# An encoder layer in f32 on one core: seven products instead of eight for a second pair in the first half of two output projections

## The chip, the cores and the metric

The kernel runs on one core of a Trainium2 chip. The core has TensorE for matrix products (PE; its weight loads are shown as PEld and overlap), VectorE (DVE), ScalarE (ACT), GpSimd (POOL), and SyncE (SP), which here issues the DMAs. Each has its own queue of instructions; semaphores tie them together. The metric is the device time of one execution in microseconds (us), as the median of several runs.

## The reference

One layer, 256 tokens (`S`), width 2048 (`D`), all in f32:

```python
x = x + 0.5 * swiglu(rms_norm(x, ffn1_norm), w_gate, w_up, w_down)      # width 5632
proj = rms_norm(x, mix_norm) @ w_in
x = x + concatenate([pool_mixer(u), gla_mixer(q, k, v, g, a_lr)]) @ w_out
x = x + mem_cross_attention(rms_norm(x, xattn_norm), rms_norm(mem, mem_norm), w_q, w_kv, w_o)
x = x + 0.5 * swiglu(rms_norm(x, ffn2_norm), w_gate, w_up, w_down)
return rms_norm(x, final_norm)
```

The last steps of mixer and attention are products of a 256 x 2048 matrix with a 2048 x 2048 one: `concatenate(...) @ w_out`, and `o @ w_o` at the end of `mem_cross_attention`. These two are called the output stages here.

## The kernel before

**Precision.** TensorE multiplies in a shortened f32 (`float32r`). Each matrix is therefore split into a high part, rounded by a copy on ACT, and a low part, the rest, by a subtraction on DVE. A product of two such matrices is three matmuls: high by high, high by low, low by high (`products`, line 336). Weights come as raw f32 by DMA and are split on the fly: a plain unit of 128 x 2048 values takes one cast of `wh` from `raw` (line 258, ACT) and one subtraction `wl` (line 259, DVE).

**Units.** The work is a stream of units (`Stream`, line 34): one load of 1 MB of weights, its split, and a function that issues its matmuls. Loads run three units ahead, splits two; `wh` and `wl` have three buffers each, `raw` three. Between units stand other operations (`st.op(f, after)`), each given as a number of units to wait. The order in which instructions are put on each engine's queue is made at build time by a scheduler that plans with estimated durations; `in_turn`, `behind_weights` and `among_weights` (lines 236 to 255) hold chosen operations in order among the weight splits on ACT and DVE.

**Seven products.** `block_s` (line 466) computes a block of 256 tokens x 1024 columns over eight pairs of 128 rows of `k`, one pair a unit. A plain unit (`unit_p`, line 506) does 2 x 2 x 2 quarter products, 24 matmuls of 128 x 512 on line 341. For a pair named in `sevens` a unit (`unit_s`, line 489) does seven quarter products in the way of Strassen and Winograd, 21 matmuls on line 462 (`seven`). It needs sums of the weight quarters and of the activation quarters:

- `split_seven` (line 424) makes three sums of weights on DVE (`T`, line 439: one of 128 x 1024, two of 128 x 512), and splits both raw quarters and sums: casts `xh` (line 258) and `wh` (line 442, two) on ACT, subtractions `xl` (line 259) and `wl` (line 443) on DVE.
- `Sums.make` (line 391) makes the sums of activations on DVE (lines 400 to 412) and splits them into `ye` and a quarter of `ys` (`split`, lines 264 and 265). It overwrites a quarter of `ys`, which `parts` hands to the seven products; plain units of that pair read `ys` as it was, so a pair's sums are made behind the last plain unit that reads it.

Four partial sums (P1, P5, P6, P7) go to two PSUM tiles of their own (`open_parts`, line 484), the others into the block's own two (`open_whole`, line 479); PSUM has four such tiles (line 100). Behind the last seven-unit `combine` (line 520) copies one of the four (line 524, ACT) and adds them up (lines 525, 526 and 529, DVE), and `merge` adds the outcome to x (line 719, twice). At the block's end the residual adds the rest to x (line 707, twice) and x goes to DRAM.

**An output stage** is one call of `into_x` (line 761): two halves of 1024 columns, `b` = 0 and 1, eight units each. It fetches the half's x, runs `block_s` with the orders and sevens of its `way`, and has two `fold`s (line 724) a half, for the 512 columns each: 16 transposes of x on PE into a `px` PSUM tile (line 730), eight scaled splits into `xs` (lines 227 on ACT, 228 on DVE), two squares (line 741). The folds of the first half run among the second half's units; those of the second half run at the start of the block that follows. `w_out` is followed by the attention's first projection, `w_o` by the second FFN.

Three ways exist (lines 755 to 759). `WHOLE` is that of four down projections in the FFNs, which have no folds; `OUTPUT` that of the two output stages; `REST` that of the FFNs' last thirds. A way is: the pairs with sums, how many units behind the call each pair's sums are made, the order of pairs in each half, and which pairs are done with seven products in each half.

Of the kernel before, what the change touches and what calls it, by code (L numbers as in the profile page):

```python
# [90 lines left out]
def build(ctx, tc, I, out):  # L91
# [651 lines left out]
    class IntoX:  # L743
# [7 lines left out]
        def make_sums(self, after=None):  # L751
            for g, n in zip(self.sums.pairs, after or self.after):
# [1 line left out]

    WHOLE = IntoX((0, 4), (2, 5), ((1, 2, 3, 5, 0, 6, 4, 7), (1, 2, 0, 3, 4, 5, 6, 7)),
                  ((0, 4), (0, 4)))
    OUTPUT = IntoX((0, 4), (0, 4), ((1, 2, 3, 4, 0, 5, 6, 7), (1, 2, 0, 3, 4, 5, 6, 7)),
                   ((0,), (0, 4)))
    REST = IntoX((0,), (2,), ((1, 2, 3, 4, 0, 5), None), ((0,), ()), False)

    def into_x(w, act, scale, gain=None, k0=0, nk=KT, spread_too=True, src=None, way=OUTPUT):

        for b in range(2):
            st.op(lambda b=b: fetch_x(b, src), 2)
            cols = wwide(w, b * 2 * NB, k0, nk)
            if way.sevens[b]:
                block_s(cols, act, way.sums, way.orders[b], residual(scale, b, 0),
                        early_parts(scale, b), way.sevens[b])
            else:
                block_t(cols, act, residual(scale, b))  # L770
            if gain is not None:
                for j in range(2):
                    st.op(lambda c=2 * b + j: fold(c, gain), 1)
        if gain is not None:
            st.op(lambda: finish_norm(4, spread_too), 2)
            if spread_too:
                st.op(spread_norm, 3)
# [426 lines left out]
        for j in range(4):  # L1204
            split_scaled(xs, 4 * c + j, v[:, j, :], gcol(G_MEM + 4 * c + j))

    OUTPUT.make_sums((1, 4))
    into_x(I["w_out"][0], ys, 1.0, G_X)
    st.op(mem_in, 2)
    for c in range(4):  # L1210
# [60 lines left out]
    def values(h):  # L1271
        for p in range(2):
            ps = ptile(uid("pv"))
            for d in range(2):
                col = slice((2 * p + d) * P, (2 * p + d + 1) * P)
                parts = [(m, a, b) for m in range(2) for a, b in ((0, 0), (0, 1), (1, 0))]
                for i, (m, a, b) in enumerate(parts):
                    nc.tensor.matmul(  # L1278
                        ps[:, d, :S], xa["V"][:, m, a, col], xa["PT"][:, m, b, :],
                        start=i == 0, stop=i == 5,  # L1280
                    )
            split_pair(ys, 4 * h + 2 * p, ps[:, :, :S])
# [6 lines left out]
    for h in range(H):  # L1289
# [4 lines left out]
        st.op(lambda h=h: values(h), 1)  # L1294
    OUTPUT.make_sums()
    into_x(w_o, ys, 1.0, G_FFN2, spread_too=False)
# [190 lines left out]
def program(shapes):  # L1487
    import concourse.bacc as _bacc

    nc = _bacc.Bacc("TRN2", target_bir_lowering=False, num_devices=1)  # L1490
    args = {
        name: nc.dram_tensor(f"in_{name}", shapes[name], F32, kind="ExternalInput").ap()
        for name in _INS
    }
    out = nc.dram_tensor("out", _OUT, F32, kind="ExternalOutput").ap()
    with tile.TileContext(nc, schedule_with_timeline_sim=True) as tc, ExitStack() as ctx:
        build(ctx, tc, args, out)
    return nc
# [10 lines left out]
```

## Time and profile before

| what | us |
|---|---|
| median of 3 runs (2095.96 to 2096.49) | 2096.08 |
| the profiled execution, in all | 2096.43 |
| its span, first to last instruction | 2094.5 |
| first load of `w_out` issued | 887.7 |
| first load of `w_o` issued | 1269.9 |

Rows of a profile read `start, duration, engine, line, operation, out<-in`, with the shape and the count; `[2.04 <-ACT wh L258]` is the idle time of the engine before the row and what ended it. Buffer numbers are left out of names: `wl` is any of its three buffers. A matmul of 128 x 512 is shown with 0.39 us, but the next starts 0.23 later, since they are pipelined and their ends are modelled. In the chain as pieces a row is `start, us, what` with the count, so us by count is what one costs. In the table of stretches, the columns are the stretch, its length, busy us and count of PE, PEld, DVE, ACT and POOL, the granted share of TensorE's clock, the DMA's busy share, and GB/s.

### The profile page before, as it was taken

How to read it: one execution, taken by the hardware profiler on the slowest of the kernel's cores; microseconds unless marked ns; L12 is line 12 of the kernel's file. 1: busy time of each engine (PE TensorE's matmuls, PEld its weight loads, DVE VectorE, ACT ScalarE, POOL GpSimd, SP SyncE). 2: the span in 40 equal slices, each digit the busy share in tenths (PEclk: the TensorE clock that was granted, in tenths of full speed). 3: DMA queues.
4: the chain of work that ended last, by engine and by line, in shares of the span. 5: the costliest groups of instructions: out<-in, count | busy, mean ns of one | idle time of the engine just before them, and what ended most of it. 6: DMA issues, size and time to landing. Idle time of an engine off the chain costs nothing.

```text
span 2094.5 us, 24553 instructions
## 1 busy us (share of the span) xinstructions
PE 2081.0 (99%) x9901; PEld 1741.6 (83%) x9901; DVE 1729.1 (83%) x1568; ACT 1115.7 (53%) x1096; POOL 14.1 (1%) x41
## 2 busy tenths in 40 slices
PE   9999999999999999999999999999999999999998
PEld 7878888888888888888888888888888888888886
DVE  7999899989998677688665555879998999989974
ACT  7654455644554555365655444556554556545544
POOL 0000000000000000000000000000000000000001
PEclk9999999999999999999999999999999999999999
DMA  7656666566656655467655555656576765676673
GB/s 262 202 199 223 240 221 209 190 224 239 223 198 236 215 179 195 151 197 266 236 181 167 172 164 167 228 190 219 182 239 209 245 205 186 222 240 222 209 255 118
DMA packets 143608, 435.94 MB, mean 208 GB/s; under 512 B 9860, under 2 KB 13544, under 8 KB 143112
## 3 DMA queue, kind: packets, MB, share of 16 engines
q1 hardware_dynamic: 143464, 434.38, 61.5%
q8 instruction: 77, 1.26, 0.2%
q14 instruction: 35, 0.29, 0.0%
q10 hardware_dynamic: 32, 0.01, 0.0%
HBM read 417.58 MB, written 16.78 MB: 207 GB/s over the span
## 4 chain that ended last, share of the span: by engine, by line
PE 93%; DVE 4%; issue 1%; ACT 1%; DMA 0%; SPq 0%; DVEq 0%
PE pt L341 44%; PE pt L462 21%; PE pa L326 15%; PE pb L341 6%; PE pe L341 3%; DVE T L439 1%; PE ph L818 1%; DVE wl L259 1%; DVE wl L443 1%; DVE xl L259 1%; PE pl L1241 1%; PE pv L1278 1%; PE px L730 1%; ACT wh L258 0%; DVE sg L539 0%
## 5 line engine op out<-in xcount | busy, mean ns | idle before, releaser
L259 DVE TENSOR_TENSOR wl<-raw,wh 128x2048 fp32r<-128x2048 f32 (+2 forms) x279 | 626.2, 2249 | 233.6 <-ACT wh L258 232.6
L258 ACT CAST wh<-raw 128x2048 fp32r<-128x2048 f32 (+2 forms) x279 | 523.3, 1880 | 339.5 <-PE pt L341 106.5
L341 PE MATMUL pt<-wh,xs 128*128 128x512 f32 x1536 | 495.0, 390 | 0.0
L341 PE MATMUL pt<-wh,ys 128*128 128x512 f32 x1360 | 427.8, 390 | 0.0
L442 ACT CAST wh<-T 128x1024 fp32r<-128x1024 f32 x206 | 216.8, 1053 | 340.0 <-DVE T L439 325.8
L341 PEld LDWEIGHTS pt<-wh,xs 128*128 128x128 f32 x1536 | 287.6, 188 | 59.4 <-ACT xs L227 0.2
L326 PE MATMUL pa<-xs,wh 128*128 128x512 f32 x896 | 315.9, 397 | 0.0
L341 PE MATMUL pt<-wl,xs 128*128 128x512 f32 x768 | 299.7, 390 | 0.0
L341 PEld LDWEIGHTS pt<-wh,ys 128*128 128x128 f32 x1360 | 255.0, 188 | 52.7
L341 PE MATMUL pt<-wl,ys 128*128 128x512 f32 x680 | 264.9, 390 | 0.0
L326 PE MATMUL pa<-xs,wl 128*128 128x256 f32 x896 | 248.3, 281 | 0.0
L443 DVE TENSOR_TENSOR wl<-T,wh 128x2048 fp32r<-128x2048 f32 x103 | 235.2, 2283 | 1.3 <-ACT wh L442 1.3
L326 PEld LDWEIGHTS pa<-xs,wh 128*128 128x128 f32 x896 | 167.6, 188 | 38.1 <-issue 0.3
L259 DVE TENSOR_TENSOR xl<-raw,xh 128x1536 fp32r<-128x1536 f32 x103 | 180.3, 1750 | 0.0
L326 PEld LDWEIGHTS pa<-xs,wl 128*128 128x128 f32 x896 | 169.1, 189 | 1.7 <-issue 0.2
L341 PEld LDWEIGHTS pt<-wl,xs 128*128 128x128 f32 x768 | 144.2, 188 | 29.8
L258 ACT CAST xh<-raw 128x1536 fp32r<-128x1536 f32 x103 | 152.3, 1479 | 10.6 <-DMA raw<-in_ffn_w_gate 8.5
L341 PEld LDWEIGHTS pt<-wl,ys 128*128 128x128 f32 x680 | 127.7, 188 | 26.2
L439 DVE TENSOR_TENSOR T<-T,raw 128x512 f32<-128x512 f32 x206 | 142.2, 690 | 5.7
L439 DVE TENSOR_TENSOR T<-raw 128x1024 f32<-128x1024 f32 x103 | 125.4, 1217 | 0.5
L462 PE MATMUL pt<-wh,xs 128*128 128x512 f32 x320 | 124.6, 389 | 0.0
L462 PE MATMUL pt<-wh,xe 128*128 128x512 f32 x320 | 124.5, 389 | 0.0
(236 smaller groups left out, 2412.6 us busy)
## 6 DMA issues: line engine op xcount, KB each, us to landing
raw<-in_ffn_w_down SPq DMA_DIRECT2D x88, 1024.0 KB, 5.5
raw<-in_ffn_w_up SPq DMA_DIRECT2D x80, 1024.0 KB, 5.0
raw<-in_ffn_w_gate SPq DMA_DIRECT2D x77, 1024.0 KB, 5.0
raw<-in_w_in SPq DMA_DIRECT2D x32, 1024.0 KB, 5.2
raw<-in_xattn_w_kv SPq DMA_DIRECT2D x32, 1024.0 KB, 5.3
raw<-in_w_out SPq DMA_DIRECT2D x16, 1024.0 KB, 5.6
raw<-in_xattn_w_q SPq DMA_DIRECT2D x16, 1024.0 KB, 5.9
raw<-in_xattn_w_o SPq DMA_DIRECT2D x16, 1024.0 KB, 5.6
```

The source lines that it names most:

```text
L258: in_turn("scalar", lambda: nc.scalar.copy(hi, src))
L259: in_turn("vector", lambda: nc.vector.tensor_tensor(out=lo, in0=src, in1=f32(hi), op=ALU.subtract))
L326: nc.tensor.matmul(o, w, x, start=k == 0 and i == 0, stop=last and i == 1)
L341: nc.tensor.matmul(ps, a, w, start=first and i == 0, stop=last and i == 2)
L439: in_turn("vector", lambda: nc.vector.tensor_tensor(out=o, in0=a, in1=b, op=ALU.add))
L442: in_turn("scalar", lambda: nc.scalar.copy(th[:, c], t[:, c]))
L443: in_turn("vector", lambda: nc.vector.tensor_tensor(out=tl, in0=t, in1=f32(th), op=ALU.subtract))
L462: nc.tensor.matmul(banks[n], x, w, start=n in fresh and j == 0, stop=n in ends and j == 2)
L730: nc.tensor.transpose(v[:, j, h * P : (h + 1) * P], x[:, h, j * P : (j + 1) * P], ident)
L818: nc.tensor.transpose(v[:, i, h * P : (h + 1) * P], g[:, h, i * P : (i + 1) * P], ident)
L1241: nc.tensor.matmul(ps[:, t, :M], ys[:, 4 * h + d, a, tok], xa["K"][:, d, b, :], start=i == 0, stop=i == 11,)
L1278: nc.tensor.matmul(ps[:, d, :S], xa["V"][:, m, a, col], xa["PT"][:, m, b, :], start=i == 0, stop=i == 5,)
```

## The change

```diff
-    OUTPUT = IntoX((0, 4), (0, 4), ((1, 2, 3, 4, 0, 5, 6, 7), (1, 2, 0, 3, 4, 5, 6, 7)),
-                   ((0,), (0, 4)))
+    OUTPUT = IntoX((0, 4), (0, 5), ((1, 2, 3, 5, 0, 6, 4, 7), (1, 2, 0, 3, 4, 5, 6, 7)),
+                   ((0, 4), (0, 4)))
...
-    OUTPUT.make_sums((1, 4))
+    OUTPUT.make_sums((1, 5))
     into_x(I["w_out"][0], ys, 1.0, G_X)
```

In the first half of both output stages pair 4 was a plain unit, the fourth; it becomes a unit of seven products, the seventh of eight. Pair 0 stays the fifth. Pair 4's sums are made one unit later, behind the fifth unit instead of the fourth; in the mixer `make_sums((1, 5))` says so, in attention the way's own `(0, 5)`. The combine of the first half, which follows the last seven-unit, comes behind the seventh unit instead of the fifth. The second half has the same order and sevens as before.

## The prediction

> **What bounds the kernel now.** I read the page's busy shares, its chain that ended last, the chain as pieces in order of time, stretches of 25 us over the mixer's output stage, then that stage instruction by instruction.
>
> ```profile
> PE 2081.0 (99%) x9901; PEld 1741.6 (83%) x9901; DVE 1729.1 (83%) x1568; ACT 1115.7 (53%) x1096; POOL 14.1 (1%) x41
> PE 93%; DVE 4%; issue 1%; ACT 1%; DMA 0%; SPq 0%; DVEq 0%
> ```
>
> PE is the bound, and the chain hardly leaves it. In the stage:
>
> ```profile
> 914.60 21.78 PE pt L341 x96
> ...
> 964.50 1.75 PE px L730 x16
> ...
> 977.60 7.48 PE pt L462 x33
> ```
>
> A product costs 21.78 / 96 = 0.227 us of PE, on line 341 or 462 (7.48 / 33 = 0.227). Sixteen transposes cost 1.75. No piece in the stage is a wait.
>
> ```profile
> 925.00:950.00 25.00, 25.00 (x112) 20.71 (x111) 23.17 (x27) 13.29 (x12) 0.00 (x0) 1.00 0.79 248
> 950.00:975.00 25.00, 25.00 (x120) 20.92 (x120) 22.55 (x20) 16.17 (x23) 0.00 (x0) 1.00 0.80 263
> ```
>
> But DVE (third busy figure) is full for 45.7 of these 50 us. It has 4.3 us to spare, against 83% over the whole span. That is what the change spends.
>
> **The change, part by part.** I count units by their place: in the first half of an output stage (first 1024 columns) the changed order makes units five and seven units of seven products, in the second half, as before, three and five. *Products.* In each of the two output stages one plain unit (8 x 3 products) becomes a unit of seven (7 x 3): 48 leave line 341, 42 come on line 462. Gain: 6 x 0.227 = **-1.36 us**. [...]
>
> *DVE work.*
>
> ```profile
> L259 DVE TENSOR_TENSOR wl<-raw,wh 128x2048 fp32r<-128x2048 f32 (+2 forms) x279 | 626.2, 2249 | 233.6 <-ACT wh L258 232.6
> ...
> L443 DVE TENSOR_TENSOR wl<-T,wh 128x2048 fp32r<-128x2048 f32 x103 | 235.2, 2283 | 1.3 <-ACT wh L442 1.3
> ...
> L259 DVE TENSOR_TENSOR xl<-raw,xh 128x1536 fp32r<-128x1536 f32 x103 | 180.3, 1750 | 0.0
> ...
> L439 DVE TENSOR_TENSOR T<-T,raw 128x512 f32<-128x512 f32 x206 | 142.2, 690 | 5.7
> L439 DVE TENSOR_TENSOR T<-raw 128x1024 f32<-128x1024 f32 x103 | 125.4, 1217 | 0.5
> ```
>
> A seven-split takes 1.22 + 2 x 0.69 + 1.75 + 2.28 = 6.63 where a plain one takes 2.25: 4.4 us more per stage, as much as was spare. ACT's extra casts lie in a queue that is busy 16 of 25 us, and no DMA is added (one fetch of x moves a load later, with half a stage to land). I cost both at nothing.
>
> *Where DVE's work lies.* The combine (lines 524 to 529) and its merge (719) move from behind unit five to behind unit seven; they cannot start before PE has finished that unit's partial sums. Behind the combine's first sum the changed DVE queue holds the merge, the two residuals (707) and the splits for units two to six of the second half, two of them seven-splits. The kernel already runs this order, instruction for instruction, in its down projections:
>
> ```profile
> 221.90 0.69 DVE L525 TENSOR_TENSOR sg<-pt,sg 128x512 f32<-128x512 f32 x1 [3.14 <-ACT sg L524]
> ...
> 246.17 2.29 DVE L259 TENSOR_TENSOR wl<-raw,wh 128x2048 fp32r<-128x2048 f32 x1
> ```
> ```profile
> 221.28 0.59 ACT L524 COPY sg<-pt 128x512 f32<-128x512 f32 x1 [4.84 <-PE pt L462]
> ```
>
> From the combine's first sum to unit six's low part there: 246.17 + 2.29 - 221.90 = 26.56 us, with no gap over 0.1. The output stages' queue has four fold instructions (line 228) among these:
>
> ```profile
> 968.75 0.87 DVE L228 SCALAR_TENSOR_TENSOR xs<-px,gains,xs 128x256 fp32r<-128x256 f32 x2
> ...
> 976.81 0.48 DVE L228 SCALAR_TENSOR_TENSOR xs<-px,gains,xs 128x256 fp32r<-128x256 f32 x1 [0.15 <-ACT xs L227]
> 979.62 2.29 DVE L259 TENSOR_TENSOR wl<-raw,wh 128x2048 fp32r<-128x2048 f32 x1 [2.33 <-ACT wh L258]
> ```
>
> 0.40 each from start to start, so DVE needs 26.56 + 1.6 = 28.15. That nothing slips past shows in the queue before:
>
> ```profile
> 949.73 2.28 DVE L259 TENSOR_TENSOR wl<-raw,wh 128x2048 fp32r<-128x2048 f32 x1
> 954.05 2.29 DVE L259 TENSOR_TENSOR wl<-raw,wh 128x2048 fp32r<-128x2048 f32 x1 [2.04 <-ACT wh L258]
> 956.26 1.22 DVE L439 TENSOR_TENSOR T<-raw 128x1024 f32<-128x1024 f32 x1
> ```
>
> For 2.04 us DVE waited for a cast while the next sum, which needs raw weights alone, stood behind. [...]
>
> *PE's cover, mixer.* In the changed instruction order 107 products and 16 transposes stand between the product that releases the combine's copy and the first that reads unit six's low part. The first sum starts 1.06 after that product's start (the product 0.40, the copy 0.59, and two hand-overs of 0.03 as between the two rows at 221), so PE arrives after 108 x 0.227 + 1.84 - 1.06 = 25.3 us (transposes 1.75, and 0.09 lost at the switch, rows at 1393 below); DVE is ready after 28.15, and 0.05 for the hand-over. Stall: **+2.85**.
>
> The down projections do not stall because PE has 24 more products to run there, in twelve pieces from the combine on:
>
> ```profile
> 221.92 8.16 PE pt L341 x36
> ...
> 248.67 2.04 PE pt L462 x9
> ```
>
> Together 127: PE came to that low part at 250.7, 2.2 us after it was there. In the output stages the four partial sums of the second half need PSUM banks that the folds hold until line 228 has read them: before, too, the 33 products of line 462 at 977.60 follow the last fold at 976.81 + 0.48. Twelve products of each seven-unit so stand behind unit six in the queue, or beside it, and cover nothing.
>
> *Attention.* Same queue, 111 products: PE arrives after 112 x 0.227 + 1.84 - 1.06 = 26.2, DVE after 28.2. Stall: **+2.0**.
>
> *The sums, later.* In the mixer the changed ACT order puts the second pair's `ye` cast behind a weight cast whose buffer PE frees at the end of unit six:
>
> ```profile
> 936.42 1.91 ACT L258 CAST wh<-raw 128x2048 fp32r<-128x2048 f32 x1 [2.45 <-PE pt L341]
> ...
> 939.41 0.51 ACT L264 CAST ye<-j 128x384 fp32r<-128x384 f32 x1 [0.89 <-DVE j L412]
> ```
>
> From that unit's last product on: 0.40 + 0.03 + 1.91 + 0.51 + 0.05, less 0.09 by which casts overlap, = 2.81, while PE starts 10 products (2.27) before one reads `ye`. Stall: **+0.55**. In attention the changed order has this cast ahead of the weight cast, and I cost it at nothing.
>
> *Start of the second FFN.* The last fold, the cast and the split behind it have no slack:
>
> ```profile
> 1392.18 1.91 PE L730 MATMUL px<-ident,x 128*128 128x128 f32 x16
> 1393.85 0.47 PE L341 MATMUL pt<-wh,xs 128*128 128x512 f32 x1
> 1394.16 0.39 PE L341 MATMUL pt<-wl,xs 128*128 128x512 f32 x1
> ```
> ```profile
> 1402.12 2.29 DVE L259 TENSOR_TENSOR wl<-raw,wh 128x2048 fp32r<-128x2048 f32 x1 [1.31 <-ACT wh L258]
> ```
> ```profile
> 1404.63 0.40 PE L341 MATMUL pt<-wl,xs 128*128 128x512 f32 x1
> ```
>
> The split ends at 1404.41, PE reads it at 1404.63: 0.17 to spare after 0.05 of hand-over. The unit is the FFN's fourth. The changed order has 40 products between these transposes and this unit where before has 45, because residual and fold come later against PE: 5 x 0.227 - 0.17 = **+0.95**.
>
> **Sum:** -1.36 + 2.85 + 2.0 + 0.55 + 0.95 = **+5.0 us**. The profiled execution (2094.5 span, 2096.43 in all) would be 2101.4; it lies 0.35 above the median 2096.08, and from that I forecast **2101.1**. Bounds of the unseen waits: below, nothing (then -1.36); above, a stall also pays a restart, for which the nearest rows are
>
> ```profile
> 141.00 0.40 PE L462 MATMUL pt<-wh,xe 128*128 128x512 f32 x1
> 142.42 0.50 PE L462 MATMUL pt<-xh,xs 128*128 128x512 f32 x1 [1.02 <-DVE sg L539]
> 142.76 0.40 PE L462 MATMUL pt<-xl,xs 128*128 128x512 f32 x1
> ```
>
> (after the wait 0.34 instead of 0.23 to the next start, and then 0.23 again), so 6 x 0.1 for some six stalls, or one more cast of 1.91 in line: up to 2103.0.
>
> **Rivals.** Some 0.2%, 4.2 us, is about what a measurement of this kernel can tell from no change.
> - *The cover holds.* If DVE reaches unit six 2.85 us earlier than I count, or PE finds 13 more products ahead of it (2.85 / 0.227), no split is late, and the FFN's start is met too: 2096.1 - 1.4 = 2094.7, not slower. For it: four halves in the down projections, in this order, without a stall. Against: the 24 products behind the folds.
> - *Only the two second halves stall*, while `ye` and the FFN's start are in time: 4.85 - 1.36 = +3.5, 2099.6, within 0.2%. For it: both are small differences of long chains.
> - *Loads late too.* DMA is busy 0.79 to 0.80 of the stage, and raw buffers are now freed later. A cast of 1.91 pushed back once in each stage: 2101.1 + 3.8 = 2104.9. Against it:
>
> ```profile
> L576 SPq DMA_DIRECT2D raw<-in_w_out x16: 367/368/384, 887.7 to 973.0; - x16
> ...
> DMA to landing us min/median/max: 5.5/5.6/5.7
> ```
>
>   Loads are issued (973.0 - 887.7) / 15 = 5.7 us apart, land within 5.7, and are used three units on, 15 us or more.
> - *Nothing is saved at all* falls away: the instruction order has the six products fewer.
>
> **How the numbers follow.** Forecast 0.71, cover holds 0.09, half the stalls 0.13, late loads 0.05, a gain beyond the six products (a stage elsewhere reordered for the better) 0.02. Slower by over 0.2%: 0.71 + 0.05 = 0.76; within: 0.22; faster: 0.02. The range goes from the half case with its two stalls a quarter too long (2099.6 - 4.85 / 4 = 2098.4) to the upper bound 2103.0, and leaves out about 0.18.
>
> **What will show it.** Right: PE waits of 0.5 to 1.5 us for `wl` and `wh` of line 259 some 27 us after the combine in both output stages, one of 1 us at the second FFN's start, one of 0.5 for `ye` in the mixer; DVE idle 2.5 to 3.5 us before line 525 and then none until the stall. Wrong: an unbroken PE through both stages, or stalls without DVE being full ahead of them (then the bank or the load is the cause). The forecast fails if the 107 products are not what PE runs in that time.

## The result, and the profile after

The changed kernel takes 2101.81 us (median of 9 runs, 2101.09 to 2103.55), against 2096.25 (9 runs, 2095.95 to 2096.67) for the kernel before on the same chip: ratio 1.0027, 95% interval 1.0018 to 1.0036. The profiled run took 2101.81 with a span of 2100.0, which is 5.5 us more than the 2094.5 of before.

From the page of the changed kernel: the span, the busy times, and the engines' shares of the chain that ended last.

```profile
span 2100.0 us, 24557 instructions
...
PE 2081.8 (99%) x9895; PEld 1739.8 (83%) x9895; DVE 1737.3 (83%) x1576; ACT 1119.4 (53%) x1100; POOL 14.2 (1%) x41
...
PE 90%; DVE 6%; issue 2%; ACT 1%; DMA 0%; SPq 0%; DVEq 0%; ACTq 0%
```

PE has 9895 instructions where it had 9901: the six products are gone. All the same PE's share of the chain fell from 93 to 90%, and VectorE's rose from 4 to 6%. The stretches of the mixer's output stage, and the one behind them (us; PE, PE's loads, VectorE, ScalarE and GpSimd busy; granted clock; DMA share; GB/s):

```profile
925.00:950.00 25.00, 24.58 (x109) 20.06 (x108) 23.09 (x25) 14.35 (x13) 0.00 (x0) 1.00 0.70 216
950.00:975.00 25.00, 24.95 (x118) 20.55 (x117) 21.70 (x20) 13.63 (x19) 0.00 (x0) 1.00 0.69 222
975.00:1000.00 25.00, 23.23 (x100) 18.35 (x99) 18.80 (x18) 12.46 (x13) 0.00 (x0) 1.00 0.88 323
```

Before, PE was busy 25.00 of 25 in the first two, and in the third as well:

```profile
975.00:1000.00 25.00, 25.00 (x112) 20.71 (x111) 17.88 (x14) 10.53 (x7) 0.00 (x0) 1.00 0.82 297
```

Now it has holes, the largest behind 975, at an unchanged clock. The chain as pieces in order of time (start, length, what):

```profile
941.94 5.00 PE pt L341 x22
...
947.01 1.92 ACT wh L258
948.92 0.42 ACT ye L264
...
978.48 2.20 DVE wl L443
980.68 2.21 DVE wl L259
982.89 0.04 issue
982.94 5.32 PE pt L341 x22
988.26 5.44 PE pt L462 x24
```

In the kernel before, the same view had nothing but PE here. Now the `ye` cast stands in the chain behind a weight cast, as forecast, and in the second half VectorE ends it, with the split of unit six (980.68) last. Behind 22 more products of line 341 follow, at 988.26, the 24 of line 462 that the folds' banks held back. The two ends of VectorE's chain, from its timeline (start, length, line, operation, shapes; in brackets idle time before and what released it):

```profile
954.89 0.69 DVE L525 TENSOR_TENSOR sg<-pt,sg 128x512 f32<-128x512 f32 x1 [3.17 <-ACT sg L524]
...
980.59 2.29 DVE L259 TENSOR_TENSOR wl<-raw,wh 128x2048 fp32r<-128x2048 f32 x1
```

It is 982.88 - 954.89 = 27.99 us long, where 28.15 were forecast, and VectorE hardly rests in it. PE around the mixer's largest stall, from its timeline:

```profile
979.31 0.39 PE L462 MATMUL pt<-xh,ye 128*128 128x512 f32 x1
980.11 0.51 PE L341 MATMUL pt<-wh,ys 128*128 128x512 f32 x1 [0.41 <-ACT wh L258]
980.73 0.50 PE L462 MATMUL pt<-wl,ys 128*128 128x512 f32 x1
...
982.94 0.50 PE L341 MATMUL pt<-wl,ys 128*128 128x512 f32 x1 [1.24 <-DVE wl L259]
983.28 0.64 PE L341 MATMUL pt<-wh,ys 128*128 128x512 f32 x2
```

From 979.31 to 983.28 PE started six products, 1.36 us of work at 0.227, in 3.97: 2.61 lost. There is more than one wait in it: first for unit six's high part (980.11, ScalarE's cast), then a short one for unit five's low part (980.73, behind VectorE's split of line 443, which ended at 980.68), then for unit six's own low part (982.94, VectorE's split). Read in the same way, as lost time against 0.227 from start to start, the other stalls are

- mixer, `ye` (at 949.38): 0.69
- mixer, unit four's low part (at 972.83): 0.32
- attention, unit six (at 1366.62 and 1368.95): 2.10
- second FFN's start (at 1409.95): 1.08

These and the 2.61 make 6.80; less 6 x 0.227 = 1.36 that is 5.44, the 5.5 of the spans. So the time is accounted for. What is not yet shown is the cause of the two largest terms: what makes unit six late.

### The profile page after: what moved, and what is told of

Same layout as the page of the kernel before. It is cut to its first block, busy times and chain, and to the rows that moved or that the text cites. A ratio compares the mean times of both kernels' runs of the same rounds, so it can differ in the third digit from the quotient of the medians.

```text
span 2100.0 us, 24557 instructions
## 1 busy us (share of the span) xinstructions
PE 2081.8 (99%) x9895; PEld 1739.8 (83%) x9895; DVE 1737.3 (83%) x1576; ACT 1119.4 (53%) x1100; POOL 14.2 (1%) x41
## 4 chain that ended last, share of the span: by engine, by line
PE 90%; DVE 6%; issue 2%; ACT 1%; DMA 0%; SPq 0%; DVEq 0%; ACTq 0%
PE pt L341 41%; PE pt L462 21%; PE pa L326 15%; PE pb L341 6%; PE pe L341 3%; DVE wl L259 1%; DVE T L439 1%; DVE wl L443 1%; PE ph L818 1%; DVE xl L259 1%; ACT wh L258 1%; PE pl L1241 1%; PE pv L1278 1%; DVE sg L539 0%; DVE xs L228 0%
## 5 line engine op out<-in xcount | busy, mean ns | idle before, releaser
L259 DVE TENSOR_TENSOR wl<-raw,wh 128x2048 fp32r<-128x2048 f32 (+2 forms) x277 | 621.8, 2250 | 230.3 <-ACT wh L258 229.5
L341 PE MATMUL pt<-wh,ys 128*128 128x512 f32 x1328 | 420.2, 390 | 0.8 <-ACT wh L258 0.8
L442 ACT CAST wh<-T 128x1024 fp32r<-128x1024 f32 x210 | 221.1, 1053 | 351.9 <-DVE T L439 345.7
L341 PEld LDWEIGHTS pt<-wh,ys 128*128 128x128 f32 x1328 | 248.9, 188 | 52.9 <-ACT wh L258 1.7
L341 PE MATMUL pt<-wl,ys 128*128 128x512 f32 x664 | 258.9, 390 | 2.4 <-DVE wl L259 2.4
L443 DVE TENSOR_TENSOR wl<-T,wh 128x2048 fp32r<-128x2048 f32 x105 | 239.9, 2285 | 0.8 <-ACT wh L442 0.8
L259 DVE TENSOR_TENSOR xl<-raw,xh 128x1536 fp32r<-128x1536 f32 x105 | 183.9, 1752 | 0.0
```

The costliest lines, as they stand in the source:

```text
L259: in_turn("vector", lambda: nc.vector.tensor_tensor(out=lo, in0=src, in1=f32(hi), op=ALU.subtract))
L341: nc.tensor.matmul(ps, a, w, start=first and i == 0, stop=last and i == 2)
L442: in_turn("scalar", lambda: nc.scalar.copy(th[:, c], t[:, c]))
L443: in_turn("vector", lambda: nc.vector.tensor_tensor(out=tl, in0=t, in1=f32(th), op=ALU.subtract))
```

## The experiments

Two theories stand. The first is the prediction's: unit six is late because VectorE's queue behind the combine is 28 us long. The second came from ScalarE's timeline of the changed kernel, where the cast that feeds unit six's split had waited for PE:

```profile
978.15 1.91 ACT L258 CAST wh<-raw 128x2048 fp32r<-128x2048 f32 x1 [1.04 <-PE pt L341]
```

By 978.15 PE has just ended unit four (its last product started at 977.72), and ScalarE was idle for 1.04 until then. There are three `wh` and three `wl` buffers. Units three and five, the units of seven, still hold theirs, since twelve products of each wait for the folds' banks (such a buffer is called pinned here); so unit six takes unit four's. The profile leaves out buffer numbers, so this is read from what ended the wait, a product of line 341, and from the order of the products. From then on cast 1.91 and split 2.29 run one after the other. In numbers: the cast ends at 980.06, so the split could end at 982.4 even on an idle VectorE; it ended at 982.88. In the attention the two ends coincide:

```profile
1364.66 1.92 ACT L258 CAST wh<-raw 128x2048 fp32r<-128x2048 f32 x1 [1.61 <-PE pt L341]
```
```profile
1364.33 2.28 DVE L443 TENSOR_TENSOR wl<-T,wh 128x2048 fp32r<-128x2048 f32 x1
1366.60 2.29 DVE L259 TENSOR_TENSOR wl<-raw,wh 128x2048 fp32r<-128x2048 f32 x1
```

The cast ends at 1366.58, and VectorE is through with the split before at 1366.61. The two theories give nearly the same stall, and the profile of the changed kernel alone can't part them.

**VectorE relieved.** The merge is left out of the first half:

```
-                        early_parts(scale, b), way.sevens[b])
+                        (lambda minus, plus: None) if way is OUTPUT and b == 0 else early_parts(scale, b),
+                        way.sevens[b])
```

> The changed kernel with the first half's merge (line 719: two operations of 1.22 us on VectorE in each output stage) left out; everything else keeps its place. The combine's four sums are still made but never reach x, so the output lacks them. Theory 1 (the prediction's: VectorE's queue behind the combine is what is late): the chain from the combine's first sum to unit six's low part falls from 28.0 to 25.5 us, PE arrives after 25.3 (mixer) and 26.2 (attention), so 2.85 and 2.0 us of stall become 0.2 and 0; with the ye stall of 0.55, at most 0.95 at the second FFN's start and -1.36 the time is 2096.4 to 2097.3 against 2096.1 before. Theory 2 (unit six's weight buffers are the bound: unit three's and five's twelve held-back products each pin their wh and wl while the folds hold the banks, so the cast of unit six waits for PE to finish unit four, and cast 1.91 plus split 2.29 then run with nothing in front of PE): VectorE being early changes at most the 0.5 us between the end of that cast and the start of its split, and the time stays 2101 to 2102, with both stalls in place and VectorE idle ahead of the split.

Measured: 2103.18 us (2102.81 to 2104.68), before 2096.43, ratio 1.0032 (1.0019 to 1.0044). The first theory's 2096.4 to 2097.3 is some 6 us off. The second's 2101 to 2102 is missed too, by 1.2, through new waits that neither theory had (below). So the time alone does not decide; the stall itself does. Unit six in the mixer, from ScalarE's, VectorE's and PE's timelines of this run:

```profile
977.83 1.91 ACT L258 CAST wh<-raw 128x2048 fp32r<-128x2048 f32 x1 [1.74 <-PE pt L341]
```
```profile
977.70 0.87 DVE L228 SCALAR_TENSOR_TENSOR xs<-px,gains,xs 128x256 fp32r<-128x256 f32 x2
979.77 2.29 DVE L259 TENSOR_TENSOR wl<-raw,wh 128x2048 fp32r<-128x2048 f32 x1 [1.21 <-ACT wh L258]
```
```profile
979.40 0.39 PE L462 MATMUL pt<-wh,ys 128*128 128x512 f32 x1
979.79 0.73 PE L341 MATMUL pt<-wh,ys 128*128 128x512 f32 x2
982.12 0.50 PE L341 MATMUL pt<-wl,ys 128*128 128x512 f32 x1 [1.59 <-DVE wl L259]
982.46 0.63 PE L341 MATMUL pt<-wh,ys 128*128 128x512 f32 x2
```

VectorE now stands idle for 1.21 us ahead of the split, waiting for the cast, and the cast still waits for PE. The stall is 982.46 - 979.40 less four products, 3.06 - 0.91 = 2.15. Taking 2.44 us out of VectorE's queue bought 0.46, no more than the half microsecond by which the split had trailed its cast. In the attention it bought nothing: there too VectorE now waits for the cast, and by the same reading the stall is 2.15 where it was 2.10.

```profile
1366.51 2.29 DVE L259 TENSOR_TENSOR wl<-raw,wh 128x2048 fp32r<-128x2048 f32 x1 [1.12 <-ACT wh L258]
```

The first theory falls with this. The kernel as a whole is no faster, since it has a new wait one unit on, at unit seven (the piece `DVE wl L259` at 991.66 in its chain, PE goes on at 994.00), of 0.98 us in each output stage, and 1.53 instead of 1.08 at the second FFN's start. Where the wait at unit seven comes from is told with the attention alone, below.

**The banks free.** The first half's two folds are left out of both output stages:

```
-            if gain is not None:
+            if gain is not None and (b or way is not OUTPUT):
                 for j in range(2):
                     st.op(lambda c=2 * b + j: fold(c, gain), 1)
```

> The changed kernel with the folds of the first half's two chunks left out of both output stages (16 transposes, 1.75 us of PE, eight operations of line 228 and their ScalarE part in each stage), so no fold holds PSUM banks while the second half starts; the four chunks of xs that the folds make keep what stood there. By work removed alone PE is about 3.5 to 3.9 us shorter in all. Theory 1 without the banks (VectorE alone): VectorE's chain is 1.6 us shorter, PE's cover 1.75 us shorter, so the stalls stay as they are, and the time is 2101.5 - 3.9 = about 2098. Theory 2 (banks, and through them the pinned buffers): the 24 held-back products run in their place, unit three's and five's buffers are freed in turn, both second-half stalls vanish, and the time is 2096.1 - 3.9 - 1.36 + 0.6 to 1.6 for the ye stall and the FFN's start = 2091.4 to 2092.5. The prediction's own account, which had both banks and queue, also says vanish here.

Measured: 2092.65 us (2091.78 to 2093.57), ratio 0.9980 (0.9971 to 0.9988), 0.15 above what the second theory gave, with a before that is 0.3 above the 2096.1 it reckoned with. Its chain through the second half of the mixer's stage, with the first and the last of thirteen pieces:

```profile
954.62 8.16 PE pt L341 x36
...
983.40 16.09 PE pt L341 x71
```

All pieces between are PE's as well; the products of line 462 run where their units stand, and no second half stalls, though VectorE's queue is only 1.45 us shorter than in the changed kernel (from 954.60 to 981.14, 26.54 us) and PE has 1.75 us less of transposes there. The stall needs the held-back products. This kernel alone doesn't say whether they matter as cover that is missing ahead of unit six or as holders of buffers. With the one before it the reading is both: where the cover is gone, the wait for a buffer decides when unit six is ready. No run gave the kernel a fourth pair of buffers, so the buffer itself was not relieved while the products stayed behind.

**One unit moved.** In the second half the second unit of seven comes one place later, so that unit five is plain:

```
-    OUTPUT = IntoX((0, 4), (0, 5), ((1, 2, 3, 5, 0, 6, 4, 7), (1, 2, 0, 3, 4, 5, 6, 7)),
+    OUTPUT = IntoX((0, 4), (0, 5), ((1, 2, 3, 5, 0, 6, 4, 7), (1, 2, 0, 3, 5, 4, 6, 7)),
```

> The changed kernel with one thing moved: in the second half the second unit of seven comes at place six instead of five (order 1, 2, 0, 3, 5, 4, 6, 7), so that unit five is plain. VectorE's work behind the combine is the same in sum; 12 products are held back by the folds' banks instead of 24, and one unit's weight buffers stay pinned instead of two. Pinned buffers: no stall at units four to seven in either stage; what is left is -1.36 + 0.69 for ye + 1.1 to 1.2 for the second FFN's start = +0.4 to +0.5 us, 2096.6 to 2096.9. VectorE's queue alone: a unit of seven still stands ahead of or at unit six, the low part of unit six is ready 28 us after the combine or later, and some 2 us in each stage stay, 2100 to 2101.

Measured: 2096.96 us (2096.28 to 2098.87), before 2096.47, ratio 1.0003 (0.9994 to 1.0011). The chain of the mixer's second half, from its pieces:

```profile
969.97 2.29 DVE wl L259
972.27 0.04 issue
972.31 10.76 PE pt L341 x46
983.07 7.48 PE pt L462 x33
990.55 5.89 PE pt L341 x26
```

The time is just above the pinned buffers' range and far from the queue's. From 972.31 on PE runs without a hole; the stalls at unit six are gone in both stages. VectorE's instructions are the same in number and kind as in the changed kernel. Since twelve products fewer are held back, there is more cover as well as one pinned buffer less; this run does not part those two. That leaves the `ye` stall, the second FFN's start, and 0.32 us at unit four, which the expectation did not have. There VectorE's queue does end the chain (969.97), and this small term is the queue's own: with the merge left out it is gone (two starts at 972.37 and 972.60 in that run).

**One stage at a time.** The change in the mixer alone, and in the attention alone; the other stage keeps the orders, sums and sevens of before. First the edit for the mixer alone, then, with the same `OUTPUT2`, that for the attention alone:

```
+    OUTPUT2 = IntoX((0, 4), (0, 4), ((1, 2, 3, 4, 0, 5, 6, 7), (1, 2, 0, 3, 4, 5, 6, 7)),
+                    ((0,), (0, 4)))
...
-    OUTPUT.make_sums()
-    into_x(w_o, ys, 1.0, G_FFN2, spread_too=False)
+    OUTPUT2.make_sums()
+    into_x(w_o, ys, 1.0, G_FFN2, spread_too=False, way=OUTPUT2)
```
```
-    OUTPUT.make_sums((1, 5))
-    into_x(I["w_out"][0], ys, 1.0, G_X)
+    OUTPUT2.make_sums((1, 4))
+    into_x(I["w_out"][0], ys, 1.0, G_X, way=OUTPUT2)
```

> The change in the mixer's output stage alone; attention's is as before. If the terms add: -0.68 for three products, +0.69 for ye, +0.32 at unit four, +2.59 at unit six = +2.9 us, 2099.0 (the prediction's terms: -0.68 + 0.55 + 2.85 = +2.7, 2098.8). Rival (what the mixer loses is partly cover that a later stage lacks, or the instruction order of the mixer depends on what follows): clearly less, +1.3 or under, 2097.4.

> The change in the attention's output stage alone; the mixer's is as before. If the terms add: -0.68 for three products, +2.09 at unit six, +1.08 at the second FFN's start = +2.5 us, 2098.6 (the prediction's terms: -0.68 + 2.0 + 0.95 = +2.3, 2098.4). No ye wait anywhere. Rival: the FFN's start is late only through the mixer's delay, then +1.4, 2097.5.

Measured, beside 2096.43: mixer alone 2099.06 (ratio 1.0013, 1.0004 to 1.0022), +2.6, near the +2.9 of the terms; attention alone 2101.12 (1.0022, 1.0013 to 1.0031), +4.7 where +2.5 was expected. The two sum to 7.3, and both together cost 5.5. Attention alone has a stall that the full change does not have. Unit seven's cast in the two kernels, from ScalarE's timelines, first the full change:

```profile
1374.33 1.91 ACT L258 CAST wh<-raw 128x2048 fp32r<-128x2048 f32 x1 [4.14 <-PE pt L341]
1377.01 1.92 ACT L258 CAST wh<-raw 128x2048 fp32r<-128x2048 f32 x1 [0.76 <-PE pt L462]
```

then attention alone, with PE's wait for it:

```profile
1374.78 1.91 ACT L258 CAST wh<-raw 128x2048 fp32r<-128x2048 f32 x1 [6.58 <-PE pt L462]
```
```profile
1379.07 0.50 PE L341 MATMUL pt<-wl,ys 128*128 128x512 f32 x1 [0.93 <-DVE wl L259]
```

In the full change unit seven's cast takes the buffer that unit six's last plain product gives back (line 341), and the unit after it takes that of a held-back product (line 462). In the other, called the second pattern below, unit seven already depends on a held-back product, and comes too late: 1.20 us lost there, and 1.53 instead of 1.08 at the FFN's start. With the +2.5 these make +4.2 of the +4.7; what the rest is stays open. The source of this stage is the same in both kernels; the instructions of line 462 stand in another order among themselves, and that order was settled when the kernel was built. So the price of pinned buffers is not one number: it depends on which buffer the next unit happens to take. The kernel without merges has the second pattern in both stages (its cast for unit seven, at 989.71, had waited for a product of line 462). What makes the build choose one or the other was not looked into.

**The sums.** Only the sums one step later, on the kernel before:

```
-    OUTPUT = IntoX((0, 4), (0, 4), ((1, 2, 3, 4, 0, 5, 6, 7), (1, 2, 0, 3, 4, 5, 6, 7)),
+    OUTPUT = IntoX((0, 4), (0, 5), ((1, 2, 3, 4, 0, 5, 6, 7), (1, 2, 0, 3, 4, 5, 6, 7)),
                    ((0,), (0, 4)))
...
-    OUTPUT.make_sums((1, 4))
+    OUTPUT.make_sums((1, 5))
```

> The kernel before, its products and orders untouched, with only the sums of the second pair one step later in both stages. If the later sums cost nothing by themselves (before's first half reads ye only at place eight or not at all, with a unit of slack): 2096.1 to 2096.4, no wait for ye. If the ye cast behind a weight cast is late whatever reads it: 0.5 to 0.7 us in the mixer, 2096.8 to 2097.1.

Measured: 2096.22 us, ratio 0.9998 (0.9989 to 1.0006): no difference that shows. And the changed kernel with its sums one step earlier again, (0, 4) and (1, 4):

> The changed kernel with the sums one step earlier again, as before the change. If the later sums are what makes the ye stall of 0.69 us, it goes, and the rest stays: 2101.1 against 2101.8 for the change. Rival: the sums' four VectorE operations and casts then lie in front of the second unit of seven's split and push that and what follows back; the ye stall goes but others grow, up to 1 us more than the change, 2102.4.

Measured: 2103.75 us (2101.93 to 2104.22), ratio 1.0032 (1.0020 to 1.0045). The `ye` stall is gone, but the stage is built in the second pattern, with the wait at unit seven in both stages; the expectation had the direction of the rival and not its size. The five runs spread over 2.3 us, and the profiled one took 2102.44, so 1.3 us of the median stand in no profile. With this second half, the earlier sums save nothing.

**A version without the stalls.** If held-back products are the cost, no unit of seven should start in the second half before the folds have given their banks back:

```
-    OUTPUT = IntoX((0, 4), (0, 5), ((1, 2, 3, 5, 0, 6, 4, 7), (1, 2, 0, 3, 4, 5, 6, 7)),
+    OUTPUT = IntoX((0, 4), (0, 4), ((1, 2, 3, 5, 0, 6, 4, 7), (1, 2, 3, 5, 0, 4, 6, 7)),
                    ((0, 4), (0, 4)))
...
-    OUTPUT.make_sums((1, 5))
+    OUTPUT.make_sums((1, 4))
```

> The changed first half (sevens at places five and seven) with a second half whose sevens stand at places five and six (order 1, 2, 3, 5, 0, 4, 6, 7), and the sums after four weights as before the change. No unit of seven starts before the folds have given their banks back, so no product is held back by them and no buffer is pinned; the sums are one step earlier, so ye is in time. If pinned buffers and the late sums are all that the change pays for: no stall in either stage, also none at the second FFN's start, and the whole -1.36 us shows: 2094.7 to 2095.1, faster than before by 0.06%. If VectorE's queue behind the combine is a bound by itself: stalls of 1 us or more in each stage stay, 2096 or more; if the earlier sums cost a stall of their own behind the second unit of seven, 2095.5 to 2097.

Measured: 2094.37 us (2093.84 to 2095.35, 11 runs), before 2096.47 (27 runs), ratio 0.9990 (0.9981 to 0.9999). All its runs lie below all of before's (2095.74 to 2098.32), though the interval ends just short of 1; the changed kernel's 2101.81 is 7.4 away. Its page, and its chain behind the first half of the mixer's stage:

```profile
PE 2078.9 (99%) x9895; PEld 1740.1 (83%) x9895; DVE 1737.0 (83%) x1576; ACT 1118.7 (53%) x1100; POOL 14.1 (1%) x41
...
PE 93%; DVE 4%; issue 1%; ACT 1%; DMA 0%; SPq 0%; DVEq 0%
```
```profile
951.62 17.24 PE pt L341 x76
968.86 1.75 PE px L730 x16
970.61 9.76 PE pt L341 x43
980.37 7.48 PE pt L462 x33
```

PE has the same products and VectorE the same 1576 instructions as in the changed kernel, and no stall is left in either stage or at the second FFN's start. The median is 2.1 us lower, the span 1.9; 1.36 of it are the six products. For the rest no cause was sought; the medians of the kernel before differ by 0.4 between sets of runs (2096.08 to 2096.47). Even here the folds' banks come late for unit five: its other twelve products start only at 983.84, behind the first seven of unit six and the last fold (line 228 ends at 982.32), but PE has work throughout. The version moves the cover, the pinned buffers and the sums at once: it shows that the stalls can be avoided, not which of the three did it.

## Why the prediction held, point by point

The time was right, 2101.1 against 2101.81, and so was the sign. For the two largest terms the size was luck, as told below. Of the steps:

- *Six products, -1.36*: right, by the instruction count.
- *VectorE's length, 28.15*: 27.99. *PE's cover without the 24 held-back products*: right, PE ran the 107 and 111 products that were counted, and the 24 stand behind unit six (988.26 in the chain above).
- *Stall in the second halves, +2.85 and +2.0*: 2.61 and 2.10, and 0.32 more in the mixer at unit four, which was not named.
- *`ye`, +0.55*: 0.69. *The FFN's start, +0.95*: 1.08. Both were short by 0.13 to 0.14, most of it the restart: behind these waits the next start came 0.34 later instead of 0.23. The prediction had this only in its upper bound. In all, -0.24 and +0.10 at unit six, +0.32, +0.14 and +0.13 bring the sum from 5.0 to 5.44.
- *Only the two second halves stall* and *loads late too*: the first falls with the stalls at `ye` and the FFN. For the second, no cast of the two stages waited for a load in the profile; the weight cast ahead of `ye` and that of unit six waited for PE.

**The step that failed** is the one that priced the second halves, as VectorE's need of 28.15 less PE's cover of 25.3 (26.2 in the attention). The cover was right, but VectorE's queue was not the only need. ScalarE was costed at nothing, from its busy time of 16 us in 25; the cast that counted was late not through ScalarE's work but because its buffer came free late. A chain over ScalarE, from PE's end of unit four through a pinned weight buffer, a cast of 1.91 and a split of 2.29, ends at 982.4, half a microsecond ahead of VectorE's own 982.88; in the attention the two end together. That the size came out right is luck: two chains end within half a microsecond of each other, and the prediction priced one. The test that the prediction set itself, VectorE full ahead of the stall, was met and showed nothing: taking 2.44 us out of the queue left 2.15 of the 2.61. For the same reason one condition of the rival *the cover holds*, VectorE 2.85 us earlier, would not have been enough. The other, 13 more products ahead of unit six, no run tested alone; the version without stalls, in which PE runs without a hole, takes 2094.37, near that rival's 2094.7.

A hint of it stood in a row that the prediction quotes: in the kernel before, the split of unit six at 979.62 had been idle 2.33 us waiting for its cast. ScalarE's timeline of before goes on to say why:

```profile
977.68 1.91 ACT L258 CAST wh<-raw 128x2048 fp32r<-128x2048 f32 x1 [0.90 <-PE pt L341]
```

The cast already waited for PE, at the same place and nearly as long (0.90 against 1.04). It cost nothing there, since 33 products of line 462 stood in front of unit six's low part, 7.48 us of cover. The change put 24 of them behind it, and the old wait came to light.

## What to carry to other kernels

When an instruction ends a chain, follow each of its inputs back, not the fullest engine: here a full queue and a pinned buffer ended within 0.5 us of each other, and relieving one of them while the other stayed told that it was not the one to work on. In this kernel the products held back for PSUM banks also held the weight buffers that they were to read, which left unit six only the buffer of unit four: its cast had waited 1.04 us when it started at 978.15. Keep work that opens new banks behind the readers that free them. And look in the kernel before for waits that are covered: a change that moves the cover pays for them.

## What the runs showed of the hardware

**The restart.** After a wait of PE the second start came 0.33 to 0.35 us after the first, where the second product waited for nothing itself (982.94 to 983.28 in the changed kernel; 982.12 to 982.46 and 994.00 to 994.35 without the merge), and then 0.23 again: 0.11 us on top of each such stall. In the changed kernel the granted clock was 1.00 there (982 to 985).

**The clock.** In the profiled run of the mixer alone, which was 2100.61 us where the median is 2099.06, PE's granted clock fell by half for one short stretch behind the stall at unit six (columns as in the windows above):

```profile
980.00:983.00 3.00, 1.65 (x5) 0.82 (x6) 3.00 (x4) 0.54 (x2) 0.00 (x0) 1.00 0.91 315
983.00:986.20 3.20, 3.20 (x9) 2.50 (x8) 1.29 (x4) 0.87 (x2) 0.00 (x0) 0.50 0.95 351
```

For 3.2 us products start some 0.427 us apart instead of 0.227 (three between 983.84 and 985.12); eight of them cost 1.6 us more. The full change has the same stall, 979.31 to 983.28, and kept a clock of 1.00 in its profiled run. The longest idle time of PE in the stall was 1.24 us in both; with the mixer alone it started four other products between the starts at 979.05 and 982.68, in the full change four between those at 979.31 and 982.94. What brought the clock down in the one run and not in the other, the two profiles do not show, nor that it was the stall. So one run with this stall paid 1.6 us behind it on top of the wait, and the other nothing; how often that happens was not measured.
